# Twelve weight preparations of a hybrid layer's mixer and second feed-forward net done during the first feed-forward net and kept in DRAM

## The chip, the cores and the metric

The kernel runs as one program on one core of a Trainium2 chip. The metric is the device time of one execution in microseconds, the median over several executions. The engines named below are TensorE (PE, its weight loads PEld), VectorE (DVE), ScalarE (ACT), GpSimd (POOL) and SyncE (SP), which here only issues DMAs. Each engine works through its own instructions in order, and waits at an instruction whose inputs or buffers are not ready.

## The reference, cut to what matters

One layer works on 528 tokens (16 learned ones and 512 of the input) of width 1024: half a SwiGLU feed-forward step of width 2816, a mixer with two branches (a diagonal state-space model, and attention over 128 selected keys), and another half feed-forward step. Everything is fp32.

```python
def swiglu(x, w_gate, w_up, w_down):
    return (jax.nn.silu(x @ w_gate) * (x @ w_up)) @ w_down

hn = rms_norm(h, ff1_norm_pre[l])
h = h + 0.5 * rms_norm(swiglu(hn, ff1_w_gate[l], ff1_w_up[l], ff1_w_down[l]), ff1_norm_post[l])
hn = rms_norm(h, mix_norm_pre[l])
proj = hn @ w_in[l]                      # 1024 x 3784
u_a, q_idx, k_idx, w_idx, q, k, v, gates = split_columns(proj, IN_SPLITS)
y_a = s5_mixer(u_a, ...)                 # state-space scan, GELU, sigmoid GLU
y_b = dsa_mixer(q_idx, k_idx, w_idx, q, k, v, rel_bias, top_k)   # index scores, top 128 keys, attention
g = jax.nn.sigmoid(gates).reshape(bsz, L, N_BRANCH, D_MODEL)
merged = g[:, :, 0] * (y_a @ w_branch_a[l]) + g[:, :, 1] * (y_b @ w_branch_b[l])
h = h + rms_norm(merged @ w_out[l], mix_norm_post[l])
hn = rms_norm(h, ff2_norm_pre[l])
h = h + 0.5 * rms_norm(swiglu(hn, ff2_w_gate[l], ff2_w_up[l], ff2_w_down[l]), ff2_norm_post[l])
```

## The kernel before

**Three products for one.** Every fp32 product runs as three f16 products. An operand is written as a high part (rounded to f16) and a low part (what the rounding left, again f16), and `mm3` (L313 to L319) adds high times high, high times low and low times high in PSUM. Weights come from DRAM as fp32 and are split on the chip. `unit` (L260 to L273) does it for one unit of weights, 1024 x 256 values: SP loads 1 MB into a staging buffer `ws` (two buffers), ACT writes the high part scaled by 256 into a tile `wh` (L271), DVE the low part (L272), both in four pieces of 128x512 or fewer larger ones. Six `wh` tiles of 1 MB (high and low) exist; a tile comes free when PE has used it.

**Stages.** The first net's gate and up products (22 column tiles of 128, in pairs that share a unit of each matrix) run from some 10 us to 272 us, its down product until about 390 us. In them `hook` is called several times in a tile, and each call from tile 4 on does one step of the set-up of attention and state-space model (L788 to L813). Then comes the mixer (to about 752 us): the projections of the index, key and value columns, and then `filler`, which gives PE the work of two query units, eight gate units, the GLU, both branch products, while the index scores, top-128 selection (DVE, L1335 and L1336), state-space scans (DVE L1244, POOL L1251, PE L1238 to L1263) and attention (PE L1304, POOL L1363, ACT L1371, PE L1379, DVE L298, PE L1411) run beside it. PE's own order is written out by hand there; the other engines' order is set by priorities when the program is built.

**The second net** (`ff2`, from about 752 us) runs its first two column tiles with plain units, and the other twenty in ten pairs with Strassen's seven products instead of eight. A pair's weights arrive as `raw` (128x4x512 of gate and of up; L95). From three of the four blocks come high and low parts `wr` (L103, L108), from sums of the blocks (`sums`, L113 to L115) high and low parts `whs`. The activations take the same treatment: `comb` (L1554 to L1572) and its parts `tops` (L298, L296). A product (L137) fills a PSUM bank with two 256-token halves; ACT copies banks out (L153: `p`, `u`).

**Queue order.** All weight loads, the copies between partitions (`kx`, `kk`, L949), the state-space model's loads (`U` L1218, `E` L1228, `R` L1230, `Tm` L1256, `Gm` L1258), the bias table `BV` (L1046) and the store `Ud` (L1028) are issued by SP, in one order.

Of the kernel before, what the change touches and what calls it, by code (L numbers as in the profile page):

```python
# [17 lines left out]
KT = 8  # L18
# [42 lines left out]
def layouts(inputs):  # L61


    import numpy as np
    out = {}
    for key in ("gate", "up"):
        w = np.asarray(inputs["ff2_w_" + key])[0].reshape(2, 4, 128, NF, 128)
        f1, f2 = w[:, :, :, 2:12], w[:, :, :, 12:22]
        q = np.stack([f2[1], f1[0], f1[1], f2[0]])
        out["ff2_%s_pairs" % key] = np.ascontiguousarray(q.transpose(3, 2, 0, 1, 4)).reshape(10, 128, 4, 512)  # L70
    return out


class Strassen:
# [14 lines left out]
    def load(self, p):  # L89
        l, nc = self.l, self.l.nc  # L90
        with l.hi():
            for i, w in enumerate(self.w):
                r = l.wst.tile([128, 4, 512], F32, tag="ws", name="raw")
                s = l.SG.tile([128, 4, 512], F32, tag="sums", name="sums", bufs=2)
                nc.sync.dma_start(r, w[p])  # L95
                self.raw[p, i], self.sums[p, i] = r, s
                self.ops[p, i] = (l.SG.tile([128, 2, 3, 512], F16, tag="wr", name="wr", bufs=4),
                                  l.whl.tile([128, 2, 4, 512], F16, tag="wh", name="whs"))

    def hi(self, p, i, b):  # L100

# [118 lines left out]
class Layer:  # L220
# [39 lines left out]
    def unit(self, w, k0, nk, c0, n, ctx=None, lead=None, parts=1, pool=None, early=False):  # L260

        nc = self.nc
        with ctx or self.hi():
            st = self.staging(early, nk, n)
            nc.sync.dma_start(st, w[k0 * 128:(k0 + nk) * 128, c0:c0 + n].rearrange("(k p) n -> p k n", p=128))
            wt = (pool or self.whl).tile([128, 2, nk, n], F16, tag="wh", name="wh")
        with ctx or (self.tc.high_priority(offset=lead) if lead else self.hi()):
            step = nk // parts
            for k in range(0, nk, step):
                ks = slice(k, k + step)  # L270
                nc.scalar.activation(wt[:, 0, ks], st[:, ks], AF.Copy, scale=WS)  # L271
                nc.vector.scalar_tensor_tensor(wt[:, 1, ks], st[:, ks], WS, wt[:, 0, ks], op0=MUL, op1=SUB)  # L272
        return wt  # L273

    def staging(self, early, nk, n):
# [587 lines left out]
    def ff1(self):  # L863
        with self.prio(SP0):
            self.start()

        def fillers():
            yield
            self.attn_setup()
            yield  # L870
            yield from self.ssm_setup()
        fill = fillers()

        def hook(ft):
            if ft >= F0:
                next(fill, None)
        with self.tc.manual_schedule(engines={mybir.EngineType.PE}) if MAN else nullcontext():
            self.ff1_gate_up(hook)
        for _ in fill:
            pass  # L880
        self.hn2 = self.hn
        self.ff1_down()
# [5 lines left out]
    def mid(self):  # L888
# [186 lines left out]
        def filler():  # L1075
            nonlocal tags

            for j2 in range(2):
                with self.after(self.norm_end) if j2 < NE else nullcontext():
                    u = self.unit(w, 0, KT, C_Q + j2 * 256, 256, lead=LEAD, parts=4)  # L1080
                for hs in REAL:
                    yield from qproj(u, 2 * j2, hs, self.q)
            tags = cycle(TG2)
            for i, t_ in enumerate((T0, T1)):
                for j4 in range(4):
                    if 4 * i + j4 == 7:
                        yield from glu()
                    with self.after(self.norm_end) if 4 * i + j4 + 2 < NE else nullcontext():
                        u = self.unit(w, 0, KT, C_G + i * D + j4 * 256, 256, lead=LEAD, parts=4)
                    for j in range(2):  # L1090
                        p = yield from proj_steps(u, unit_cols(u, j), (NM, T))
                        with self.hi():
                            s.activation(t_[:, 2 * j4 + j], p, AF.Tanh, scale=0.5 * IWS)
# [408 lines left out]
    def ff2(self):  # L1502
# [7 lines left out]

        ug, uu = [self.unit(w, 0, KT, 0, 256, parts=F2P) for w in (wg, wu)]
        sg.load(0)
        manual = lambda: self.tc.manual_schedule(engines={mybir.EngineType.PE, mybir.EngineType.DVE, mybir.EngineType.Activation})
        pgs = [[self.ps("ps"), self.ps("sc")] for j in range(2)]

# [7 lines left out]
        for j in range(2):  # L1523
            prod(j, 128, SEQ)
        with self.prio(WP), self.after(self.wout_marks[0]), manual():
            for i in range(2):
                sg.hi(0, i, 0)
            sg.lo(0, 0, 0)
            for _ in self.wout_T(0):
                pass  # L1530
            sg.lo(0, 1, 0)
        self.sctx.close()
        self.lctx_close()
        self.kctx, self.cctx = ExitStack(), ExitStack()
# [48 lines left out]
            self.split(t_[:, 0], t_[:, 1], sl)  # L1583
        sg.rest = rest
        with manual():
            sg.add(0, 0)
            sg.hi(0, 0, 1)
            sg.add(0, 1)
            sg.hi(0, 1, 1)
            sg.load(1)  # L1590
            combine(0, 1)
            for i in range(2):
                sg.lo(0, i, 1)
            for j in range(2):
                prod(j, 0, 128)
                s.activation(sl[:, j], pgs[j][0], AF.Silu, scale=IWS)
# [67 lines left out]

SSMW = 512
SH = 2
NS=((0,1),1,1,3,3)
NE = 3
LN=0b0110110
# [63 lines left out]
```

## Time and profile before

| what | value |
|---|---|
| device time, median of 3 runs | 1098.4 us (1096.31 to 1099.3) |
| profiled execution, device time | 1100.52 us |
| its span (first to last instruction) | 1098.7 us |
| PE busy | 1046.6 us (95%), 8382 matmuls |
| DVE, ACT, POOL busy | 755.1 us (69%), 471.0 us (43%), 173.4 us (16%) |
| mean granted PE clock | 0.98 |
| chain that ended last | PE 76%, DVE 14%, ACT 4%, DMA 2% |
| bytes moved by DMA | 135.37 MB, mean 123 GB/s |

The profiled execution is 1.82 us longer than its span. Busy shares are means over stages with different limits; a matmul's end is modelled, and a busy PE can be one at the lower of its two clocks (1.2 instead of 2.4 GHz), which the granted clock beside a stretch shows: 1.00 is full, 0.5 half. An idle time in a row stands in brackets with what ended it.

### The profile page before, as it was taken

Reading aid. Unit: us, or ns where it says so; the run is one execution under the profiler, and the core shown is the slowest. Engines: PE = TensorE matmul, PEld = TensorE weight load, DVE = VectorE, ACT = ScalarE, POOL = GpSimd, SP = SyncE. Lnnn points to the kernel's source line nnn. Section 1 sums busy time; section 2 is a strip of 40 time slices with the busy share of each in tenths; the row PEclk is TensorE's granted clock in tenths of the full one; section 3 lists DMA queues with packets and bytes.
Section 4 is the critical chain, followed back from the end, with each engine's and each line's share of the span. In section 5 each row is a group of like instructions: output and inputs, shape, how many; then the busy total and the mean of one; then the engine's idle time right before and its main releaser. Section 6 shows DMA issues by size and latency. Waiting matters only on the chain.

```text
span 1098.7 us, 20502 instructions
## 1 busy us (share of the span) xinstructions
PE 1046.6 (95%) x8382; PEld 790.3 (72%) x8382; DVE 755.1 (69%) x1598; ACT 471.0 (43%) x854; POOL 173.4 (16%) x258
## 2 busy tenths in 40 slices
PE   7999999999999999889998999999889999999996
PEld 6888888888888988676654456565678888864443
DVE  7749766678222585599987986579979999952222
ACT  6634333333222265555656553334445555632200
POOL 4400133300000231046430223210000000001000
PEclk9999999999999999899998999999889999999999
DMA  8654454433333055946313225121323333365011
GB/s 274 184 157 144 137 176 142 140 102 127 123 106 97 1 152 169 272 155 165 126 57 99 69 78 180 51 87 69 116 78 116 116 116 116 116 219 203 20 39 39
DMA packets 94478, 135.37 MB, mean 123 GB/s; under 512 B 17336, under 2 KB 69192, under 8 KB 91824
## 3 DMA queue, kind: packets, MB, share of 16 engines
q1 hardware_dynamic: 88704, 119.92, 34.3%
q0 software_dynamic: 5056, 13.08, 4.1%
q8 instruction: 66, 1.08, 0.4%
q10 hardware_dynamic: 624, 1.06, 0.3%
q14 instruction: 28, 0.23, 0.1%
HBM read 118.45 MB, written 19.05 MB: 125 GB/s over the span
## 4 chain that ended last, share of the span: by engine, by line
PE 76%; DVE 14%; ACT 4%; DMA 2%; issue 2%; POOL 1%; SPq 1%; DVEq 0%; ACTq 0%; POOLq 0%
PE psps L319 11%; PE psps L317 11%; PE psps L315 11%; PE psps L137 9%; PE scps L315 7%; PE scps L319 7%; PE scps L317 7%; PE ptps L137 4%; DVE wh L272 3%; PE avps L137 2%; DVE iacc L1336 1%; PE ptps L319 1%; PE ptps L317 1%; PE ptps L315 1%; DVE m L1335 1%
## 5 line engine op out<-in xcount | busy, mean ns | idle before, releaser
L272 DVE SCALAR_TENSOR_TENSOR wh<-ws,wh 128x512 f16<-128x512 f32 (+2 forms) x176 | 167.2, 986 | 91.5 <-ACT wh L271 91.0
L319 PEld LDWEIGHTS <-wh 128*128 128x128 f16 x1616 | 159.3, 99 | 45.5 <-issue 4.5
L315 PEld LDWEIGHTS <-wh 128*128 128x128 f16 x1616 | 159.2, 99 | 42.0 <-issue 6.0
L317 PEld LDWEIGHTS <-wh 128*128 128x128 f16 x1616 | 159.4, 99 | 37.8 <-issue 4.5
L271 ACT ACTIVATE wh<-ws 128x512 f16<-128x512 f32 (+2 forms) x176 | 134.4, 826 | 104.7 <-PE scps L319 54.6
L315 PE MATMUL psps<-hn,wh 128*128 128x256 f16 (+2 forms) x640 | 166.0, 302 | 4.2 <-DVE kk L300 1.9
L317 PE MATMUL psps<-hn,wh 128*128 128x256 f16 (+2 forms) x640 | 166.5, 302 | 1.1 <-POOL hn L298 0.6
L319 PE MATMUL psps<-hn,wh 128*128 128x256 f16 (+2 forms) x640 | 166.5, 301 | 0.0
L137 PEld LDWEIGHTS <-whs 128*128 128x128 f16 x960 | 95.0, 99 | 18.0 <-issue 5.9
L137 PEld LDWEIGHTS <-wr 128*128 128x128 f16 x720 | 71.8, 100 | 13.5 <-issue 3.7
L315 PE MATMUL scps<-hn,wh 128*128 128x272 f16 (+1 forms) x344 | 68.7, 276 | 0.0
L317 PE MATMUL scps<-hn,wh 128*128 128x272 f16 (+1 forms) x344 | 68.6, 276 | 0.0
L319 PE MATMUL scps<-hn,wh 128*128 128x272 f16 (+1 forms) x344 | 68.1, 276 | 0.0
L137 PE MATMUL psps<-tops,whs 128*128 128x256 f16 x480 | 57.8, 279 | 5.5 <-ACT u L153 5.5
L108 DVE SCALAR_TENSOR_TENSOR whs<-sums,whs 128x2048 f16<-128x2048 f32 x20 | 45.7, 2291 | 3.6 <-ACT whs L103 3.6
L510 ACT ACTIVATE sl<-scps 128x272 f32<-128x272 f32 (+1 forms) x40 | 14.4, 386 | 66.5 <-PE scps L319 66.5
L103 ACT ACTIVATE whs<-sums 128x2048 f16<-128x2048 f32 x20 | 38.1, 1904 | 10.2 <-DVE sums L115 10.2
L1363 POOL TENSOR_TENSOR BM<-BV,iacc 128x272 f32<-128x272 f32 (+1 forms) x32 | 28.8, 909 | 85.0 <-DVE asm L1369 73.5
L315 PE MATMUL psps<-h,wh 128*128 128x256 f16 (+1 forms) x176 | 41.5, 276 | 0.0
L317 PE MATMUL psps<-h,wh 128*128 128x256 f16 (+1 forms) x176 | 41.5, 276 | 0.0
L319 PE MATMUL psps<-h,wh 128*128 128x256 f16 (+1 forms) x176 | 41.5, 276 | 0.0
L319 PE MATMUL scps<-h,wh 128*128 128x256 f16 (+1 forms) x176 | 41.5, 276 | 0.0
(412 smaller groups left out, 2125.5 us busy)
## 6 DMA issues: line engine op xcount, KB each, us to landing
ws<-in_ff_w_down_dram SPq DMA_DIRECT2D x18, 1024.0 KB, 5.2
ws<-in_w_in_dram SPq DMA_DIRECT2D x14, 1024.0 KB, 6.6
ws<-in_ff_w_gate_dram SPq DMA_DIRECT2D x10, 1024.0 KB, 5.4
ws<-in_ff_w_up_dram SPq DMA_DIRECT2D x10, 1024.0 KB, 6.2
raw<-ff_gate_pairs SPq DMA_DIRECT2D x10, 1024.0 KB, 4.8
raw<-ff_up_pairs SPq DMA_DIRECT2D x10, 1024.0 KB, 4.9
ws<-in_w_out_dram SPq DMA_DIRECT2D x4, 1024.0 KB, 5.1
ws<-in_ff_w_down_dram SPq DMA_DIRECT2D x4, 768.0 KB, 4.7
```

The costliest lines, as they stand in the source:

```text
L103: self.l.nc.scalar.activation(self.ops[p, i][b][:, 0], src[:, 0:3] if b == 0 else src, AF.Copy, scale=WS)
L108: self.l.nc.vector.scalar_tensor_tensor(o[:, 1], src[:, 0:3] if b == 0 else src, WS, o[:, 0], op0=MUL, op1=SUB)
L137: mm(out, a, b[:, kt], start=first and i == kt == x == 0, stop=kt == 3 and x == 2, skip_group_check=True)
L271: nc.scalar.activation(wt[:, 0, ks], st[:, ks], AF.Copy, scale=WS)
L272: nc.vector.scalar_tensor_tensor(wt[:, 1, ks], st[:, ks], WS, wt[:, 0, ks], op0=MUL, op1=SUB)
L315: mm(p, a[0], bh, start=first, stop=False)
L317: mm(p, a[0], bl, start=False, stop=False)
L319: mm(p, a[1], bh, start=False, stop=last)
L510: s.activation(sl[:, a:b], p[:, :b - a], AF.Silu, scale=IWS)
L1335: v.max(m8, work)
L1336: v.match_replace(work, m8, work, -3e38)
L1363: nc.gpsimd.tensor_add(BM[:, :w], self.BV[:, h, NA - w:], madd[:, f:])
```

## The change

Ten units of the mixer's weights (two of the query, eight of the gates; `AHEAD`), until now loaded and split in the mixer, and the first Strassen pair of the second net (gate and up: blocks and sums), until now loaded, summed and split at that net's start, are loaded and split during the first net's gate and up products. `ahead_steps` does it, one step at every second call of `hook` from tile 4 on: load into a buffer `wa` (two buffers, in the pool `EX` that holds the first net's early units), split by ACT and DVE in pieces of 128x1024 (128x512 for `wr`), and store the f16 parts to a tile `wd` in DRAM. The ten units come from a new input, `ahead`, that holds each of them as 8 KB in one piece for each partition. All twelve loads and fourteen stores are issued by SP; a load is issued only after the weight load that the program issued last before it (`sp_mark`).

In the mixer `kept_unit` takes the place of `unit`: one load of 1 MB f16 from `wd` into a `wh` tile, and no work of ACT or DVE. In the second net `load(0)` loads the four prepared tiles (two `wr` of 0.75 MB, two `whs` of 1 MB), and the splits and sums of pair 0 go. `load(1)`, the raw weights of the next pair, is issued directly behind it.

```diff
@@ layouts
-    out = {}
+    w = np.asarray(inputs["w_in"])[0].reshape(KT, 128, -1)
+    out = {"ahead": np.stack([w[:, :, c:c + 256].transpose(1, 0, 2) for c in AHEAD])}
@@ Strassen.load
             for i, w in enumerate(self.w):
+                self.ops[p, i] = (l.SG.tile([128, 2, 3, 512], F16, tag="wr", name="wr", bufs=4),
+                                  l.whl.tile([128, 2, 4, 512], F16, tag="wh", name="whs"))
+                if p == 0:
+                    for b in range(2):
+                        nc.sync.dma_start(self.ops[p, i][b], l.kept[i, b])
+                    continue
...
-                self.ops[p, i] = (l.SG.tile([128, 2, 3, 512], F16, tag="wr", name="wr", bufs=4),
-                                  l.whl.tile([128, 2, 4, 512], F16, tag="wh", name="whs"))
@@ Layer.unit
-            nc.sync.dma_start(st, w[k0 * 128:(k0 + nk) * 128, c0:c0 + n].rearrange("(k p) n -> p k n", p=128))
+            self.sp_mark = nc.sync.dma_start(st, w[k0 * 128:(k0 + nk) * 128, c0:c0 + n].rearrange("(k p) n -> p k n", p=128))
@@ new
+    def ahead_steps(self):
...
+        def halves(dst, src, step):
+            for a in range(0, src.shape[1], step):
+                ks = slice(a, a + step)
+                nc.scalar.activation(dst[:, 0, ks], src[:, ks], AF.Copy, scale=WS)
+                nc.vector.scalar_tensor_tensor(dst[:, 1, ks], src[:, ks], WS, dst[:, 0, ks], op0=MUL, op1=SUB)
+
+        def keep(key, t_):
+            self.kept[key] = d = self.dp.tile(list(t_.shape), F16, tag=str(key), name="wd")
+            nc.sync.dma_start(d, t_)
+
+        def stage(shape, src=None, dt=F32):
+            t_ = self.EX.tile(shape, dt, tag="wh", name="wa")
+            if src is not None:
+                with self.after([self.sp_mark]):
+                    nc.sync.dma_start(t_, src)
+            return t_
+        for i, c in enumerate(AHEAD):
+            st = stage([128, KT, 256], self.I["ahead"][i])
+            wt = stage([128, 2, KT, 256], dt=F16)
+            halves(wt, st, 4)
+            keep(c, wt)
+            yield
+        v = nc.vector
+        for i, key in enumerate(("gate", "up")):
+            r = stage([128, 4, 512], self.I[f"ff2_{key}_pairs"][0])
+            wr = stage([128, 2, 3, 512], dt=F16)
+            halves(wr, r[:, 0:3], 1)
+            keep((i, 0), wr)
+            yield
+            t_ = stage([128, 4, 512])
+            v.tensor_add(t_[:, 0:2], r[:, 3:4].to_broadcast([128, 2, 512]), r[:, 0:2])
+            v.tensor_add(t_[:, 2], t_[:, 0], r[:, 1])
+            v.tensor_add(t_[:, 3], t_[:, 2], r[:, 2])
+            yield
+            whs = stage([128, 2, 4, 512], dt=F16)
+            halves(whs, t_, 2)
+            keep((i, 1), whs)
+            yield
+
+    def kept_unit(self, c):
+        with self.hi():
+            wt = self.whl.tile([128, 2, KT, 256], F16, tag="wh", name="wh")
+            self.nc.sync.dma_start(wt, self.kept[c])
+        return wt
@@ ff1
         def hook(ft):
             if ft >= F0:
                 next(fill, None)
+                if next(calls) % 2:
+                    next(ahead, None)
@@ filler
-                    u = self.unit(w, 0, KT, C_Q + j2 * 256, 256, lead=LEAD, parts=4)
+                    u = self.kept_unit(C_Q + j2 * 256)
...
-                        u = self.unit(w, 0, KT, C_G + i * D + j4 * 256, 256, lead=LEAD, parts=4)
+                        u = self.kept_unit(C_G + i * D + j4 * 256)
@@ ff2
         sg.load(0)
+        sg.load(1)
...
-            for i in range(2):
-                sg.hi(0, i, 0)
-            sg.lo(0, 0, 0)
             for _ in self.wout_T(0):
                 pass
-            sg.lo(0, 1, 0)
...
-            sg.add(0, 0)
-            sg.hi(0, 0, 1)
-            sg.add(0, 1)
-            sg.hi(0, 1, 1)
-            sg.load(1)
             combine(0, 1)
-            for i in range(2):
-                sg.lo(0, i, 1)
@@ constants
+AHEAD = [C_Q, C_Q + 256] + [C_G + i * 256 for i in range(8)]
```

Line numbers of the changed kernel are 5 higher than before in the Strassen class, 55 in `split` (L298 is L353), and 59 to 62 higher in the mixer and the second net.

The first place is SP's order where the last projections end, about 438 to 460 us of the profile before. `Ud`, `BV`, `R`, `Tm` and `Gm` serve the state-space model and the attention bias, `kx` and `kk` are copies to other partitions, `U` the model's inputs, `ws` a raw weight unit. Before:

```order
L1046 DMA BV<-Vr 128x8x272
L1028 DMA Ud<-uT 128x528
L1230 DMA R<-Rd 128x528
L1256 DMA Tm<-Td 128x512
L1258 DMA Gm<-Gd 128x512
L949 DMA kx<-kx 64x2x256
L265 DMA ws<-in_w_in_dram 128x8x256
L949 DMA kk<-kk 64x2x256
L1218 DMA U<-Ud 16x32x66 x8
```

After (`wh<-wd` is the load of a prepared unit):

```order
L1318 DMA Tm<-Td 128x512
L1320 DMA Gm<-Gd 128x512
L1090 DMA Ud<-uT 128x528
L1108 DMA BV<-Vr 128x8x272
L1090 DMA Ud<-uT 128x528
L327 DMA wh<-wd 128x4096
L1011 DMA kx<-kx 64x2x256
L1011 DMA kk<-kk 64x2x256
L1280 DMA U<-Ud 16x32x66 x5
L327 DMA wh<-wd 128x4096
```

The raw load that stood behind `kx` is gone and a prepared unit's load stands in front of it; `R`, `Tm` and `Gm` stand further ahead, `BV` nearer, and another prepared unit's load stands between the loads of `U`.

The second place is DVE's order in the mixer, about 476 to 485 us: `Vbd` of the state-space model, the selection (`MAX`, `MATCH_REPLACE` on `iacc`), the query's evacuation `q`, the low part of a weight unit, and the scan `SZ`. Before:

```order
L1167 TENSOR_TENSOR Vbd<-ptps,mask 128x512
L1325 MEMSET iacc 64x64
L1335 MAX m_5939<-iacc 128x8
L961 SCALAR_TENSOR_TENSOR q<-psps,q 64x256
L272 SCALAR_TENSOR_TENSOR wh<-ws,wh 128x512
L1336 MATCH_REPLACE iacc<-m_5939,iacc 128x528
L272 SCALAR_TENSOR_TENSOR wh<-ws,wh 128x512 x3
L1335 MAX m_5970<-iacc 128x8
L961 SCALAR_TENSOR_TENSOR q<-psps,q 64x256
L1336 MATCH_REPLACE iacc<-m_5970,iacc 128x528
L961 SCALAR_TENSOR_TENSOR q<-psps,q 64x256
L1244 SCALAR_TENSOR_TENSOR SZ<-dec,SZ 128x264
```

After:

```order
L1387 MEMSET iacc 64x64
L1229 TENSOR_TENSOR Vbd<-ptps,mask 128x512
L1397 MAX m_6064<-iacc 128x8
L1023 SCALAR_TENSOR_TENSOR q<-psps,q 64x256
L1398 MATCH_REPLACE iacc<-m_6064,iacc 128x528
L1023 SCALAR_TENSOR_TENSOR q<-psps,q 64x256
L1397 MAX m_6086<-iacc 128x8
L1398 MATCH_REPLACE iacc<-m_6086,iacc 128x528
L1397 MAX m_6141<-iacc 128x8
L1398 MATCH_REPLACE iacc<-m_6141,iacc 128x528
L1306 SCALAR_TENSOR_TENSOR SZ<-dec,SZ 128x264
```

The four passes over a weight unit (rows `wh<-ws,wh`) are gone from in front of the scan, and three more steps of the selection stand there.

The third place is DVE's order at the start of the second net, from about 770 us. Before:

```order
L108 SCALAR_TENSOR_TENSOR wr<-raw,wr 128x1536
L298 TENSOR_TENSOR hf<-ptps,hf 128x4x128 x2
L108 SCALAR_TENSOR_TENSOR wr<-raw,wr 128x1536
L1554 TENSOR_TENSOR raw<-hf 128x4x128
L298 TENSOR_TENSOR tops<-comb,tops 128x4x128 x5
L1565 SCALAR_TENSOR_TENSOR comb<-comb,raw 128x4x128
L298 TENSOR_TENSOR tops<-comb,tops 128x4x128
L108 SCALAR_TENSOR_TENSOR whs<-sums,whs 128x2048 x2
L1568 TENSOR_TENSOR comb<-raw 128x4x128
L113 TENSOR_TENSOR sums<-raw 128x1024
L298 TENSOR_TENSOR tops<-comb,tops 128x4x128
```

After:

```order
L353 TENSOR_TENSOR hf<-ptps,hf 128x4x128 x2
L1613 TENSOR_TENSOR raw<-hf 128x4x128
L353 TENSOR_TENSOR tops<-comb,tops 128x4x128 x2
L1624 SCALAR_TENSOR_TENSOR comb<-comb,raw 128x4x128
L353 TENSOR_TENSOR tops<-comb,tops 128x4x128 x4
L1627 TENSOR_TENSOR comb<-raw 128x4x128
L353 TENSOR_TENSOR tops<-comb,tops 128x4x128
L113 SCALAR_TENSOR_TENSOR wr<-raw,wr 128x1536 x2
L1613 TENSOR_TENSOR raw<-hf 128x4x128
L185 TENSOR_TENSOR C<-avps,p_9557 128x512
L118 TENSOR_TENSOR sums<-raw 128x1024
L1631 SCALAR_TENSOR_TENSOR comb<-comb,raw 128x4x128
```

The passes that write the first pair's `wr` and `whs` are gone; the first `comb` stands behind two `tops` passes instead of five, and the passes over `wr` that remain are the second pair's.

## Rows read from the trace of the kernel before

**Rows 1.** Windows of the span: start:end, length, busy per engine, granted clock, DMA share, GB/s.

```profile
60.00:192.00 132.00, 132.00 (x1160) 112.05 (x1158) 88.99 (x234) 47.38 (x100) 25.49 (x43) 1.00 0.47 149
385.00:466.00 81.00, 74.19 (x720) 64.31 (x719) 53.23 (x127) 45.73 (x110) 13.21 (x18) 0.96 0.71 199
466.00:568.00 102.00, 94.33 (x696) 66.29 (x694) 98.07 (x211) 57.82 (x134) 49.13 (x72) 0.98 0.44 135
568.00:640.00 72.00, 62.45 (x366) 32.80 (x367) 59.59 (x139) 42.28 (x83) 15.84 (x22) 0.91 0.28 82
...
752.00:806.00 54.00, 43.68 (x340) 31.68 (x339) 45.11 (x71) 25.74 (x32) 0.00 (x0) 0.87 0.25 90
```

**Rows 2.** PE's waits, 466 to 568 us: waited for, total us, times, longest.

```profile
PE ptps L1263 <- POOL SZ L1251: 2.6, 1, 2.6
PE ptps L1262 <- DVE PT L298: 2.3, 2, 1.4
PE ptps L1262 <- DVE Vbd L1167: 0.7, 1, 0.7
PE psps L315 <- DVE q L961: 0.6, 1, 0.6
```

**Rows 3.** Timeline of DVE, 476 to 490 us: start, us, what.

```profile
479.10 3.54 DVE L272 SCALAR_TENSOR_TENSOR wh<-ws,wh 128x512 f16<-128x512 f32 x3
...
485.00 0.71 DVE L1244 TENSOR_TENSOR_SCAN SZ<-dec,SZ 128x264 f32<-128x264 f32 x1
```

**Rows 4.** Groups by line, 466 to 568 us: busy, mean ns, idle before.

```profile
L272 DVE SCALAR_TENSOR_TENSOR wh<-ws,wh 128x512 f16<-128x512 f32 x24 | 20.8, 911 | 0.0
```

**Rows 5.** PE's waits, 385 to 466 us.

```profile
PE scps L1304 <- DMA kx<-kx: 2.1, 1, 2.1
PE psps L315 <- DVE kk L300: 1.9, 2, 1.4
```

**Rows 6.** Chain that ended last, 436 to 452 us: start, us, what.

```profile
438.90 2.50 DVE wh L272 x4
...
442.00 7.57 DMA kx<-kx
```

**Rows 7.** PE's waits, 752 to 806 us.

```profile
PE psps L137 <- ACT u L153: 5.0, 1, 5.0
PE psps L137 <- ACT sl L1596: 3.6, 1, 3.6
```

**Rows 8.** Timeline of DVE, start of the second net.

```profile
770.39 1.75 DVE L108 SCALAR_TENSOR_TENSOR wr<-raw,wr 128x1536 f16<-128x1536 f32 x1
...
780.76 4.49 DVE L108 SCALAR_TENSOR_TENSOR whs<-sums,whs 128x2048 f16<-128x2048 f32 x2
...
796.80 0.68 DVE L1572 SCALAR_TENSOR_TENSOR comb<-comb,raw 128x512 f32<-128x512 f32 x1
```

**Rows 9.** Timeline of ACT, start of the second net.

```profile
779.49 0.63 ACT L296 ACTIVATE tops<-comb 128x512 f16<-128x512 f32 x1 [4.15 <-DVE comb L1565]
...
797.52 0.63 ACT L296 ACTIVATE tops<-comb 128x512 f16<-128x512 f32 x1 [3.30 <-DVE comb L1572]
798.12 1.91 ACT L103 ACTIVATE whs<-sums 128x2048 f16<-128x2048 f32 x1
```

**Rows 10.** Windows: two after PE's waits, one full of DVE, one full of DMA.

```profile
781.00:788.00 7.00, 5.92 (x29) 4.12 (x29) 5.99 (x4) 2.11 (x5) 0.00 (x0) 0.51 0.02 4
798.00:805.50 7.50, 4.93 (x26) 3.61 (x26) 2.89 (x3) 2.52 (x4) 0.00 (x0) 0.54 0.39 140
82.50:110.00 27.50, 27.50 (x246) 23.84 (x245) 27.09 (x118) 12.56 (x27) 0.81 (x1) 1.00 0.44 143
432.50:447.50 15.00, 13.64 (x124) 11.88 (x123) 6.44 (x13) 7.09 (x17) 0.45 (x2) 1.00 1.03 359
```

**Rows 11.** Groups by line, first net (0 to 385 us).

```profile
L272 DVE SCALAR_TENSOR_TENSOR wh<-ws,wh 128x512 f16<-128x512 f32 x72 | 46.8, 688 | 11.1 <-ACT wh L271 11.0
```

**Rows 12.** Groups by line, mixer (385 to 760 us).

```profile
L272 DVE SCALAR_TENSOR_TENSOR wh<-ws,wh 128x1024 f16<-128x1024 f32 x8 | 9.9, 1258 | 2.5 <-ACT wh L271 2.5
```

More of the change, by code (lines that the diff above doesn't have):

```diff
@@ L272, in unit @@
                 nc.vector.scalar_tensor_tensor(wt[:, 1, ks], st[:, ks], WS, wt[:, 0, ks], op0=MUL, op1=SUB)
+        return wt
+    def ahead_steps(self):
+        nc = self.nc
+        self.kept = {}
+        def halves(dst, src, step):
[38 more added lines that the diff above has]
+            self.nc.sync.dma_start(wt, self.kept[c])
         return wt
@@ L872, in ff1 @@
         fill = fillers()
+        ahead = self.ahead_steps()
+        calls = iter(range(1000))
         def hook(ft):
@@ L879, in ff1 @@
         for _ in fill:
+            pass
+        for _ in ahead:
             pass
```

## The prediction

> **What bounds the kernel now.** I read the windows of the span first, because they show which engine fills which stage [rows 1]. Between 60 and 192 us PE never stops at full clock, and DVE has 132 - 89.0 = 43.0 us free: there PE alone sets the time. From 466 to 568 us DVE is busy 98.1 of 102 us, and PE, which still has work, stands for 102 - 94.3 = 7.7 us. From 752 to 806 us PE stands for 54 - 43.7 = 10.3 us. So a pass taken off DVE is worth nothing in the first net and may be worth something in the other two. Second come PE's waits in these stretches. In the mixer they end with DVE or with POOL's part of the scan [rows 2]; at the second net's start they end with ACT, in two gaps of 3.6 and 5.0 us [rows 7]. Third come the timelines of DVE and ACT at these waits, which show what is queued ahead of the instruction that PE waits for [rows 3, 8, 9], and last the granted clock behind the gaps: 0.51 and 0.54 in the two stretches after the second net's gaps, which is about the lower of its two levels (1.2 of 2.4 GHz) [rows 10].
>
> **Added in the first net.** Ten units in two pieces of 128x1024 give 20 passes on DVE, the two `whs` 4 more: 24 x 1.258 = 30.2 us [rows 12]. The two `wr` give 6 passes of 128x512 at 0.688 = 4.1 us [rows 11]. The sums, for each matrix one addition of 128x1024 and two of 128x512, I take at the same two durations: 2 x (1.258 + 2 x 0.688) = 5.3 us. Together 39.6 us. The steps run over about 16 tiles, some 165 us, and of the 39.6 us about 33 fall between 60 and 192 us, where 43.0 are free [rows 1]. ACT gets 30 passes, at no more than DVE's durations 34 us, against 132 - 47.4 = 84.6 us free in that window alone. DMA gets 12 loads of 1 MB and 14 stores, 12.6 and 14.2 MB: 26.7 MB in 165 us are 162 GB/s on top of 149 [rows 1], 311 in all, while 359 were moved for 15 us on end in the mixer [rows 10]. PE gets nothing. What hides all this is that PE's tiles need DVE only now and then: between 82.5 and 110 us DVE is busy 27.1 of 27.5 us, and PE does not stop once [rows 10]. If the cover is gone, PE stands for a silu or an evacuation that comes late. No row shows both loads at once. The lower bound is 0 (PE is never idle there, so nothing can be gained), the upper some two late steps of 3 us each, 6; I take 1, near the row in which DVE is full and PE doesn't wait.
>
> **Mixer, 385 to 466 us.** Five of the ten units are split here. One stall of PE, 1.4 us of the 1.9 us for `kk` [rows 5], has four passes of L272, 2.50 us, directly before it on the chain [rows 6]. Without them `kk` is ready at the pace of ACT; I take 0.9 off this stall and 0.5 off a smaller one of the same kind, -1.4. The wait for `kx` (2.1 us) stays: it is a DMA that landed 7.57 us after its issue [rows 5, 6], and in SP's order a 1 MB load of a prepared unit now stands directly ahead of it, where the raw load stood behind. Bounds: at 359 GB/s [rows 10] the 1.05 MB take 2.9 us, so at worst +2.9; at best the wait goes, -2.1. The three `R`, `Tm` and `Gm` loads that were issued just before it stand further ahead now, so I take 0.
>
> The Trainium skill (DMA: Bandwidth & Descriptors, Queues, rings and completion order) says that each DMA engine takes the descriptors of a queue in ring order, so the megabyte ahead would be moved before `kx`. By that rule alone the sum would be 2.9 us higher; the trace shows the long landing of `kx` behind the `BV` load, which agrees, but not which share each transfer ahead of it has.
>
> **Mixer, 466 to 568 us.** Of 24 passes of L272 (20.8 us) [rows 4] 20 belong to kept units and go; four are the GLU's. 20 x 0.911 = 18.2 us, by which DVE's 98.1 fall to 80, while PE's own work takes 94. DVE no longer is the bound. How this reaches PE is seen at the largest wait, 2.6 us for `SZ` [rows 2]: three passes of L272, 3.54 us, stood on DVE between 479.1 and 482.6, ahead of the scan at 485.0 [rows 3]. The four waits sum to 6.2 us. I leave 0.7 of them, since a transpose must still follow its exponential, and take 5.5. The clock granted was 0.98 of 102 us, so 2.0 us went with it, after the gaps; these go too. -7.5. Bounds: 0 (other waits replace them all) and -9.7 (all of PE's idle time and the clock).
>
> **568 to 752 us** keep their work: the splits there belong to the branch and output units, which are not prepared. 0; a gain is possible through a lead of DVE (below).
>
> **Second net's start.** The first gap ends with `sl` on ACT [rows 7], which follows a `tops` that had waited 4.15 us for `comb` L1565 [rows 9]. On DVE two passes over `wr` of 1.75 us stood ahead of that `comb` [rows 8], as the order before shows. Without them it ends 3.5 us earlier, and the gap of 3.6 closes. The second gap, 5.0 us, ends with `u`, which follows the second pair's `whs` (1.91) and a `tops` that waited 3.30 for `comb` L1572 at 796.80 [rows 8, 9]. Ahead of that on DVE the two `whs` passes go, 4.49 us [rows 8]. So `u`, which could start at 798.12 + 1.91 = 800.0, moves ahead by 3.5 + 4.5 = 8.0, to 792.0. PE went on about half a microsecond behind it, so its gap of 5.0 began at 795.5; freed of the first gap (3.6) and of its slow stretch (5.92 x 0.49 = 2.9) [rows 10], it gets there at 795.5 - 6.5 = 789.0. A gap of 2 to 3.5 us is left, since what remains ahead of `u` is the second pair's own work. PE thus goes on 8.0 us earlier, or 9.5 if the shorter `tops` queue in the new order helps as well. After a gap of two the slow stretch behind it (4.93 x 0.46 = 2.3) gets shorter by some 0.5. I take -9.0; bounds -13 (both gaps of 8.6 and both slow stretches of 5.2 gone, less 0.8 of smaller ones that appear) and -3 (the second gap grows by what the first loses and its stretch stays slow, leaving 2.9). The loads must be there: 3.7 MB from 752 us on, at 359 GB/s 10.2 us, and the first is needed at about 778.
>
> **Sum.** +1 - 1.4 + 0 - 7.5 + 0 - 9.0 = -16.9. The profiled execution took 1100.52 us, so 1083.6 for its like; it is 2.1 above the median of the runs, 1098.4, from which 1081.5 follows. I say **1082 us**.
>
> **Rivals.**
> *Only the second net gains.* In the mixer the waits move: DVE's selections follow one another through scores that come from PE, and with L272 gone PE may stand for POOL's part of `SZ` or for `kx` instead. For it speaks that the largest wait in rows 2 names POOL; against it that DVE was full. 1098.4 + 1 - 9.0 = 1090 us.
> *DVE's lead carries on.* DVE saves 18 us before 568 and PE takes 7.5 of them; if the rest lets the attention's exponentials and transposes come early, the 72 - 62.5 = 9.5 us of PE's idle time between 568 and 640 and its clock's 0.09 x 72 = 6.5 go [rows 1]: 16 us more, 1066 us. Against it: these waits lie in a chain that begins with PE's own scores.
> *Slower: late steps in the first net.* ACT and DVE take their passes in order. A pass over `wa` that waits for its load stands ahead of a tile's silu, and the silu frees PE's bank. A tile takes 11 us (132 us hold 1160 matmuls of 96 a tile), so half a tile, 5.5 us, is cover. A load that lands as late as `kx` did, 7.57 us [rows 6], lets PE stand for 2.1 us, and in the proportion of the gap of 3.6 with its slow stretch of 2.9 that costs 3.7. The gains are 17.9 without this term; from 6 such steps of 16 on the kernel is slower by over 0.3%, and with 12 it takes 1098.4 - 17.9 + 44.4 = 1125 us. For it: SP issues the loads one after another with the stores, and a store that waits for DVE holds the next load back. Against it: loads of 1 MB and passes over them already run in this stretch with PE never idle.
> *No change.* The loads from DRAM wait on SP for `wh` tiles that PE frees late, and hold `kx`, `U`, `Tm` and `Gm` and the second net's weights back by what DVE gains: about 1098 us. The order of SP speaks for it, and that PE stands for `kx` already; against it, that SP had such waits for staging buffers before.
>
> **How the numbers follow.** Forecast 0.56, its own range 1074 to 1089; only the second net 0.18; DVE's lead 0.12; late steps 0.08; no change 0.06. A range of 1066 to 1094 leaves out the last two cases, 0.14, and a little of the edges. About 0.3% (3.3 us) is what a measurement of this kernel can tell from no change. Faster by more: 0.56 + 0.18 + 0.12 = 0.86, less 0.02 for the first net's cost rising to its bound while the mixer gains nothing, 0.84. Within: 0.08. Slower: 0.08.
>
> **What would show it.** In the profile after: PE busy without a gap from 60 to 385 us (first step), DVE near 122 of 132 us there; the wait for `kk` under 1 us and that for `kx` about 2; DVE near 80 of 102 us in the stretch that answers to 466 to 568, with PE's waits for `SZ` and `PT` nearly gone; no wait for `sl`, and one of 2 to 3.5 us for `u`, in the second net. I am wrong if PE waits on evacuations in the first net, if its waits in the mixer keep their sum under other names, or if the second net starts with a wait for `wr<-wd`.

## The result, and the profile after

The changed kernel takes 1092.5 us (median of 19 executions, 1086.8 to 1096.4), the kernel before on the same chips 1102.1 us. The ratio is 0.9921 with a 95% interval of 0.9901 to 0.9941: 8.7 us faster, where 16.9 were forecast. About half of the gain is missing; the sign and the range held. (Two of the 19 executions of the kernel before took 2189 and 6158 us; without them its median is 1099.3 us, and the ratio leaves them out.)

First the windows of the kernel after that answer to [rows 1]; the columns are the same (length; busy of PE, PEld, DVE, ACT, POOL; granted clock, DMA share, GB/s).

```profile
60.00:192.00 132.00, 126.53 (x1103) 106.36 (x1101) 105.65 (x243) 66.99 (x121) 21.52 (x36) 1.00 0.86 293
385.00:466.00 81.00, 75.71 (x742) 66.27 (x741) 41.37 (x126) 31.95 (x80) 11.98 (x17) 0.96 0.66 184
466.00:568.00 102.00, 95.23 (x683) 69.22 (x682) 76.26 (x173) 48.56 (x117) 43.17 (x67) 0.92 0.45 137
568.00:640.00 72.00, 63.13 (x396) 33.69 (x394) 61.05 (x149) 41.43 (x78) 17.30 (x22) 0.98 0.26 81
752.00:806.00 54.00, 50.22 (x404) 36.40 (x403) 41.37 (x80) 21.82 (x35) 0.00 (x0) 0.97 0.36 127
```

DVE has what the change promised: 76.3 instead of 98.1 us in the third row. PE has not: it now stands 5.5 us between 60 and 192 us, where it never stood before, and in the third row its idle time fell only from 7.7 to 6.8 us, with a granted clock of 0.92 instead of 0.98. The last row is as forecast: 3.8 us idle instead of 10.3, clock 0.97 instead of 0.87.

The windows of two kernels that run apart don't hold the same work. Three waits of PE that both have serve as marks: the first `kk` (start of the mixer), a product over the last attention block (`ybh`), and a `u` behind the second net's start. The kernel before (start, duration, what, and in brackets the idle time ahead of it):

```profile
410.10 0.28 PE L315 MATMUL psps<-hn,wh 128*128 128x256 f16 x1 [0.57 <-DVE kk L300]
...
723.28 0.22 PE L315 MATMUL psps<-ybh,wh 128*128 128x128 f16 x1 [0.72 <-DVE y L1480]
...
821.65 1.58 PE L137 MATMUL psps<-tops,whs 128*128 128x256 f16 x13 [0.47 <-ACT u L153]
```

and after:

```profile
417.88 0.28 PE L370 MATMUL psps<-hn,wh 128*128 128x256 f16 x1 [0.58 <-DVE kk L355]
...
729.01 0.22 PE L370 MATMUL psps<-ybh,wh 128*128 128x128 f16 x1 [0.72 <-DVE y L1542]
...
817.59 1.58 PE L142 MATMUL psps<-tops,whs 128*128 128x256 f16 x13 [0.48 <-ACT u L158]
```

At the first mark the kernel is 7.8 us late, at the second 5.7, at the third 4.1 us early. So this execution lost 7.8 us in the first net, gained 2.1 in the mixer and 9.8 at the second net's start. In the forecast these were +1, -8.9 and -9.0. (It took 1096.4 us, the longest of the 19; the second profile below gives +7.3, -6.4 and -11.5.)

**The first net.** PE's waits from 60 to 385 us (waited for, total, times, longest), of which the kernel before has none:

```profile
PE avps L849 <- ACT B L867: 4.6, 4, 1.9
PE avps L849 <- DVE A L845: 0.8, 1, 0.8
```

They make 5.4 of the 7.8 us; the rest stays open. One of them on the timelines of SP, PE, ACT and PE again:

```profile
144.04 0.43 SPq L299 DMA_DIRECT2D wa<-ahead  x1
```

```profile
145.81 1.05 PE L861 MATMUL avps<-B,A 128*16 128x128 f32 x8
```

```profile
154.53 2.00 ACT L288 ACTIVATE wa<-wa 128x1024 f16<-128x1024 f32 x2 [6.02 <-DMA wa<-ahead]
156.44 0.57 ACT L867 ACTIVATE B<-avps 16x512 f32<-16x512 f32 x1
```

```profile
157.06 0.66 PE L849 MATMUL avps<-ident,A 128*128 128x128 f32 x4 [1.89 <-ACT B L867]
```

The load into `wa` was issued at 144.0 us. ACT stood at the pass over it from 148.5 until the load had landed at 154.5, 10.5 us after its issue. Behind the pass in ACT's order is `B`, the copy out of PSUM of the state-space model's set-up. Its input was there from 146.9 us on, when PE's product (L861) ended, but it ran only when the pass was done. PE's next set-up step, transposes (L849) into the only bank of their kind (`av`), stands in PE's order between the tile's matmuls, was reached at 155.2 us and waits for `B`. So PE stops for the set-up, not for an operand of its tile. At all four waits for `B` a pass over `wa`, for whose load ACT had stood 2.7 to 6.0 us, ends directly before `B` on ACT. The fifth wait is DVE's: its sum `A` (L845) at 119.5 us comes behind two passes over `wa` (2.35 us).

**The mixer.** PE's waits from 440 to 560 us after, for [rows 2, 5]:

```profile
PE scps L1366 <- DMA kx<-kx: 4.1, 1, 4.1
PE psps L370 <- DVE q L1023: 3.6, 1, 3.6
PE ptps L1324 <- DVE PT L353: 1.4, 1, 1.4
PE ptps L1300 <- DMA wh<-wd: 1.3, 1, 1.3
```

The waits for `SZ`, `Vbd` and `kk` that were to go are gone or small, but `kx` has doubled, and one wait of 3.6 us for `q` has come. On the chain `kx` landed later after its issue than before [rows 6]:

```profile
446.56 10.65 DMA kx<-kx
```

**The second net.** Both waits of [rows 7] are answered by one line (waits of PE, 752 to 820 us); no wait for `sl` is left:

```profile
PE psps L142 <- ACT u L158: 2.5, 2, 2.0
```

### The profile page after: what moved, and what is told of

Same layout as the page of the kernel before. It is cut to its first block, busy times and chain, and to the rows that moved or that the text cites. A ratio compares the mean times of both kernels' runs of the same rounds, so it can differ in the third digit from the quotient of the medians.

```text
span 1094.6 us, 20517 instructions
## 1 busy us (share of the span) xinstructions
PE 1044.6 (95%) x8382; PEld 790.5 (72%) x8382; DVE 747.5 (68%) x1584; ACT 471.0 (43%) x840; POOL 170.3 (16%) x258
## 4 chain that ended last, share of the span: by engine, by line
PE 62%; DVE 12%; ACT 3%; DMA 2%; issue 2%; POOL 1%; SPq 0%; DVEq 0%; ACTq 0%; POOLq 0%
PE psps L374 9%; PE psps L372 9%; PE psps L370 9%; PE psps L142 9%; PE scps L372 5%; PE scps L374 5%; PE scps L370 5%; PE ptps L142 4%; PE avps L142 2%; DVE wh L277 2%; DVE iacc L1398 1%; DVE m L1397 1%; PE scps L1366 1%; DMA kx<-kx 1%; PE ptps L374 1%
## 5 line engine op out<-in xcount | busy, mean ns | idle before, releaser
L277 DVE SCALAR_TENSOR_TENSOR wh<-ws,wh 128x512 f16<-128x512 f32 (+2 forms) x136 | 136.7, 1036 | 79.3 <-ACT wh L276 79.2
L276 ACT ACTIVATE wh<-ws 128x512 f16<-128x512 f32 (+2 forms) x136 | 112.6, 883 | 89.2 <-PE scps L374 55.1
L289 DVE SCALAR_TENSOR_TENSOR wa<-wa 128x1024 f16<-128x1024 f32 (+1 forms) x30 | 32.5, 1113 | 29.7 <-ACT wa L288 29.7
L288 ACT ACTIVATE wa<-wa 128x1024 f16<-128x1024 f32 (+1 forms) x30 | 27.4, 963 | 41.8 <-DMA wa<-ahead 27.4
L113 DVE SCALAR_TENSOR_TENSOR whs<-sums,whs 128x2048 f16<-128x2048 f32 x18 | 41.2, 2292 | 3.6 <-ACT whs L108 3.6
L370 PE MATMUL scps<-h,wh 128*128 128x256 f16 (+1 forms) x176 | 41.4, 276 | 0.0
L372 PE MATMUL scps<-h,wh 128*128 128x256 f16 (+1 forms) x176 | 41.4, 276 | 0.0
```

The lines of the kernel that those rows point to most:

```text
L113: self.l.nc.vector.scalar_tensor_tensor(o[:, 1], src[:, 0:3] if b == 0 else src, WS, o[:, 0], op0=MUL, op1=SUB)
L288: nc.scalar.activation(dst[:, 0, ks], src[:, ks], AF.Copy, scale=WS)
L289: nc.vector.scalar_tensor_tensor(dst[:, 1, ks], src[:, ks], WS, dst[:, 0, ks], op0=MUL, op1=SUB)
L370: mm(p, a[0], bh, start=first, stop=False)
L372: mm(p, a[0], bl, start=False, stop=False)
```

## The experiments

Each kernel is compared with executions of the kernel before on the same chip. In the expectations ORDER is the theory that the lost gain lies in what stands ahead of what; its rivals have other names from case to case.

**Once more.** The changed kernel as it is, for a second profile.

> The changed kernel once more, unchanged. Theory ORDER (the lost gain is a matter of what stands ahead of what in the engines' and SP's fixed orders): the same waits come back, four or five for the set-up's copies B and A between 110 and 190 us (5 us in all), kx about 4 us, q about 3.6 us with a stretch at half the clock behind it, u about 2 us; ratio to the kernel before 0.990 to 0.994. Theory CHANCE (the profiled execution, 1096.4 us, was one of the slow ones): some of these waits are absent or the slow stretch behind q is shorter than 5 us, and the profiled execution takes 1087 to 1093 us.

Measured: 1090.3 us, ratio 0.9904 (0.9876 to 0.9932); the profiled execution 1089.9. The waits for `B` and `A` came back (3.4 and 1.8 us), `kx` with 4.1, `q` with 3.6, `u` with 2.0. What differs is the clock behind the wait for `q`. Windows of the first profile after that wait:

```profile
500.00:504.00 4.00, 2.81 (x7) 1.02 (x8) 3.81 (x8) 0.67 (x2) 1.73 (x3) 0.52 0.65 244
504.00:508.00 4.00, 4.00 (x18) 3.49 (x17) 3.83 (x9) 1.14 (x3) 0.00 (x0) 0.50 0.02 4
508.00:512.00 4.00, 4.00 (x16) 2.76 (x16) 1.79 (x5) 1.26 (x4) 2.49 (x4) 0.50 0.43 141
```

and of the second:

```profile
500.00:504.00 4.00, 2.47 (x7) 0.96 (x8) 3.77 (x10) 0.98 (x3) 2.06 (x3) 0.74 0.73 274
504.00:508.00 4.00, 4.00 (x29) 3.38 (x28) 3.83 (x9) 1.19 (x4) 0.54 (x1) 0.84 0.15 44
508.00:512.00 4.00, 4.00 (x20) 1.85 (x19) 2.73 (x6) 1.80 (x4) 2.58 (x5) 1.00 0.44 153
```

The same gap of 3.6 us was followed by 12 us at half the clock in one execution; in the other the first two windows, 0.74 and 0.84, make some 3.4 us at half the clock, an estimate from these two means. The mixer, between the first two marks (306.8 instead of 313.2 us), gains 6.4 us in the second profile. The second net's start gains 11.5 us there and 9.8 in the first profile, in which the clock from 792 to 800 us was 0.82 (1.00 in the second). ORDER has the waits and the ratio right, and CHANCE the profiled time and the shorter slow stretch. The waits are the program's; a part of the spread from 1087 to 1096 us is how long the clock stays down.

**The first net's part alone.**

```diff
-                    u = self.kept_unit(C_Q + j2 * 256)
+                    u = self.unit(w, 0, KT, C_Q + j2 * 256, 256, lead=LEAD, parts=4)
...
-                        u = self.kept_unit(C_G + i * D + j4 * 256)
+                        u = self.unit(w, 0, KT, C_G + i * D + j4 * 256, 256, lead=LEAD, parts=4)
@@ Strassen.load and ff2: as before the change
```

> Everything that the change adds in the first net (loads, passes, stores, in the changed kernel's order) and nothing that it takes off: mixer and second net load and split their own weights as before, and what was stored is not used. Theory ORDER: the waits for the set-up's copies come back (about 5 us) and the first net ends some 7 us late: ratio to before 1.004 to 1.008. The prediction's term (1 us, at most 6): ratio 1.000 to 1.003.

Measured: 1107.8 us, ratio 1.0065 (1.0044 to 1.0086): +7.2 us. Its waits of PE from 60 to 385 us:

```profile
PE avps L845 <- ACT B L863: 3.0, 2, 2.0
PE avps L845 <- DVE A L841: 1.6, 1, 1.6
```

Behind the second wait for `B`, 1.95 us long, the clock fell as well:

```profile
158.00:162.00 4.00, 4.00 (x23) 2.87 (x22) 4.00 (x8) 2.24 (x5) 1.86 (x3) 0.57 0.68 231
```

This prices the term that the prediction put at 1 us and bounded at 6. The waits are 4.6 us of it. By the marks the loss is where the work was added: +8.1 us at the first, -0.3 in the mixer. The second net's start, with the code of the kernel before, took 1.7 us less than there, so that stretch differs by as much from one profile to another without the change.

**Only the ten units.** `ahead_steps` without its second loop; `Strassen.load` and `ff2` as before.

> Only the ten mixer units are prepared ahead; the second net's first pair is loaded, summed and split there, as before. Theory ORDER: the second net loses its 9.8 us again, the first net keeps three of its waits for B and A (about 4 us), the mixer gains some 2 us: ratio to the kernel before 0.998 to 1.004. Theory of the prediction: the mixer gains 8.9 and the first net loses 1: ratio 0.993.

Measured: 1097.9 us, ratio 0.9967 (0.9948 to 0.9987), between the two theories: a little better than ORDER's nearer end, 0.998, and short of the prediction's 0.993. The first mark comes 6.5 us late, the second 0.5, so the mixer gains 6.0, where ORDER had 2 and the prediction 8.9. At the second net's start both of PE's waits are back:

```profile
PE psps L138 <- ACT u L154: 5.3, 1, 5.3
PE psps L138 <- ACT sl L1654: 3.6, 1, 3.6
```

**Only the first pair.** `AHEAD = []`, and `unit` in the mixer.

> Only the second net's first pair is prepared ahead (six steps); the mixer's units are loaded and split there, as before. Theory ORDER: second net -9.8 us, first net 0 to +2, mixer 0: ratio 0.991 to 0.993, as good as the whole change. If the mixer's part of the change were worth 9 us, this would be slower than the whole change by 0.5% or more.

Measured: 1093.8 us, ratio 0.9930 (0.9903 to 0.9956), as theory ORDER had it: the first pair alone, two of the twelve preparations, is not to be told from the whole change. Its first mark is 2.7 us late and its second 3.8, and the second net's start gains 9.9 us, as in the whole change. The ten units alone had lost in the first net (6.5 us) what they gained in the mixer (6.0).

**ACT's passes behind the set-up's copy.** The same loads, passes and stores; an edge puts both halves of a pass over a prepared unit, ACT's and DVE's, behind the set-up's last copy.

```diff
+        self.kmark = None
+
         def halves(dst, src, step):
+            with self.after([self.kmark] if self.kmark else []):
+                halves_(dst, src, step)
...
-            s.activation(kev, p[:M], AF.Copy)
+            self.kmark = s.activation(kev, p[:M], AF.Copy)
```

> The whole change, but ACT's passes over a prepared unit are issued behind the copy B that the set-up emitted last, instead of ahead of it; loads, stores and passes are the same. Theory ORDER: the waits for B between 110 and 190 us (5 us idle) fall under 1 us, and the kernel is 5 to 7 us faster than the changed one: ratio to before 0.984 to 0.988. Theory TRAFFIC (the 27 MB more of DMA delay what the first net needs, whatever the order): the time stays within 1 us of the changed kernel's, ratio 0.990 to 0.994.

Measured: 1084.2 us, ratio 0.9845 (0.9812 to 0.9878). The traffic is that of the changed kernel and PE doesn't stop in this window:

```profile
60.00:192.00 132.00, 132.00 (x1161) 112.39 (x1159) 109.75 (x251) 66.90 (x121) 23.31 (x39) 1.00 0.83 285
```

Its only wait of PE from 60 to 385 us is:

```profile
PE avps L867 <- ACT A L856: 0.9, 1, 0.9
```

ACT still stands at passes over `wa` for the ten units' loads, 19.8 us from 60 to 240 us (24.3 in the changed kernel), but nothing that PE needs soon is behind them. So theory TRAFFIC falls: 285 GB/s in that window cost PE nothing by themselves. The edge moved more than it names, since PE's order in the first net is set by priorities when the program is built: the set-up's transposes stand 11.5 to 12.3 us apart on PE (12.3 before the change) instead of 8.4 to 15.6. How much of the gain beyond the named waits comes from that was not separated. This version beats both kernels. Its gain, 17 us, is close to the forecast of 16.9 in part by luck: by the marks its parts are +2.4, -6.9 and -11.5 us, where +1, -8.9 and -9.0 were forecast.

**Loads behind `kx` and `U`.** On top of that kernel; the gate units' loads get an edge behind `kk`'s copy and the last `U` load.

```diff
-                        u = self.kept_unit(C_G + i * D + j4 * 256)
+                        with self.after([m for m in (self.kk_mark, self.u_mark) if m]):
+                            u = self.kept_unit(C_G + i * D + j4 * 256)
```

> On top of the kernel in which ACT's passes stand behind the set-up's copy: the loads of the eight prepared gate units are issued by SP behind the copies kx and kk and behind all eight loads U, instead of one ahead of kx and one between the U loads. Theory ORDER: kx lands 7 to 8 us after its issue instead of over 10, its wait falls from 3.9 to 1 to 2 us, the wait of 2.0 us at the first product of U to under 1; with the slow stretch behind the first, 3 to 5 us less than 1084, so 1079 to 1081. Theory BANDWIDTH (these bytes must be moved in the same microseconds in any order): one wait is replaced by another for a gate unit, and the time stays at 1083 to 1085.

Measured: 1083.4 us, ratio 0.9833 (0.9809 to 0.9857), not to be told from 0.9845. `kx`'s wait fell from 3.9 to 2.9, that at the first product of `U` from 2.0 to 0.7:

```profile
PE psps L376 <- DVE q L1029: 3.5, 1, 3.5
PE scps L1374 <- DMA kx<-kx: 2.9, 1, 2.9
...
PE ptps L1308 <- DMA wh<-wd: 0.7, 1, 0.7
```

The copy itself came as ORDER had it, 7.4 us after its issue (7 to 8 expected) instead of 11.1 without the edit; PE, whose order moved too, was at its product 3 us earlier and so still waited:

```profile
440.25 0.60 SPq L1017 DMA_DIRECT2D kx<-kx  x1
447.67 0.55 PE L1374 MATMUL scps<-kx,qx 128*128 128x272 f16 x2 [2.86 <-DMA kx<-kx]
```

In its chain a store `Ud` takes `kx`'s place, with 10.2 us to its landing. The profiled execution is 4 us shorter than that of the kernel without the edit (span 1078.7 for 1082.7), but the median moves by 0.8. By the times BANDWIDTH is nearer, by the landing and the wait for `U` ORDER; what the edit is worth stays open.

**The scan's copies on POOL.**

```diff
-            s.activation(S[0:64, 1], S[64:128, 0], AF.Copy, scale=-1.0)
-            s.activation(S[64:128, 1], S[0:64, 0], AF.Copy)
+            nc.gpsimd.tensor_scalar(S[0:64, 1], S[64:128, 0], -1.0, None, op0=MUL)
+            nc.gpsimd.tensor_copy(S[64:128, 1], S[0:64, 0])
```

> On top of the same kernel: the two copies of the scan's state SZ that follow the scan are made by POOL instead of ACT. In ACT's order they stand ahead of a query's evacuation q and wait there for DVE's scan. Theory ORDER: the wait of 3.6 us for q falls to 0.5 to 1.5 us and the slow stretch behind it goes: 3 to 5 us less than 1084. Theory DVE (DVE is full with the selection between 480 and 500 us, and q waits for DVE itself): the wait stays at 3 us or more, and the time within 1 us.

Measured: 1084.1 us, ratio 0.9849 (0.9823 to 0.9876). The time is as theory DVE had it; the wait for `q` fits neither theory. It shrinks by a microsecond and PE stands for `SZ` instead:

```profile
PE psps L376 <- DVE q L1029: 2.6, 1, 2.6
...
PE ptps L1331 <- POOL SZ L1319: 1.7, 2, 1.0
```

What is left of the wait can be read on ACT and DVE. ACT's half of `q` is done at 490.3 us and DVE's half begins 3.0 us later, behind selection passes and the scan, without idle time on DVE between them:

```profile
489.91 0.38 ACT L1028 ACTIVATE q<-psps 64x256 f16<-64x256 f32 x1 [0.92 <-PE psps L380]
491.97 0.70 DVE L1312 TENSOR_TENSOR_SCAN SZ<-dec,SZ 128x264 f32<-128x264 f32 x1
493.30 0.42 DVE L1029 SCALAR_TENSOR_TENSOR q<-psps,q 64x256 f16<-64x256 f32 x1
```

**Both edits.**

> Both edits together with the passes behind the set-up's copy. If both theories ORDER hold, 6 to 9 us less than 1084: 1075 to 1078, ratio to before 0.976 to 0.979. If BANDWIDTH and DVE hold: 1083 to 1085.

Measured: 1084.9 us, ratio 0.9846 (0.9824 to 0.9867): no gain, as BANDWIDTH and DVE had it.

**Half the selection.** `for r in range(8 if b == 3 else (out or TOPK) // 8)`, which leaves out 64 of the 128 keys for the last 128 queries.

> On top of the kernel with ACT's passes behind the set-up's copy: the selection for the last 128 queries makes 8 of its 16 rounds (64 keys instead of 128 chosen), some 12 us of DVE less between 475 and 505 us. Theory DVE (the selection fills DVE there and q waits behind it): the wait of 3.6 us for q falls to under 1 us, DVE has idle time from 488 to 500 us, and the time falls by 3 us or more under 1084. Theory CHAIN (q waits for ACT and the scan, not for DVE's work): the wait stays at 2.5 us or more.

Measured: 1087.0 us, ratio 0.9873 (0.9845 to 0.9901). The wait for `q` is still 2.9 us:

```profile
PE psps L376 <- DVE q L1029: 2.9, 1, 2.9
```

DVE is busy 3.8 of 4 us from 488 to 492 and not at all from 496 to 500: the rounds that stand ahead of `q` in its order still stand there, and it runs dry afterwards. How much DVE has to do in all is not what holds `q`, but what stands ahead of `q` there; theory DVE falls in the form in which I had put it, and the wait is as CHAIN had it. Of the 2.9 us by which its profiled execution is longer, 1.7 lie at the second net's start, with a clock of 0.79 from 784 to 792 us (1.00 in the kernel without the edit); the 1.9 us in the mixer are not explained.

**More of PE's other work beside the selection.** `RF = 1.8` for 1.4.

> On top of the same kernel: PE gets 1.8 instead of 1.4 us of projection work for each round of the selection in the order that is written out for it, so that its work before 505 us is longer. If DVE's selection sets the pace there, the wait for q shrinks by what PE has more to do, and PE stands later instead, between 568 and 640 us, for the exponentials: time 1082 to 1087. If q's wait is a chain's latency: wait unchanged, time 1084.

Measured: 1089.6 us, ratio 0.9892 (0.9866 to 0.9918). The wait for `q` falls to 0.7 us, but from 560 to 640 us PE stands 9.5 instead of 3.7 us for the exponentials, and 4.1 for the index scores' copies:

```profile
PE ptps L1447 <- ACT Pt L1439: 9.5, 3, 4.5
PE scps L1372 <- ACT rl L1386: 4.1, 3, 2.2
```

The waits move as expected, but the time is longer than either theory allowed. PE's projections cover one wait or the other; spent early, they are missing late.

## Why the prediction was wrong, step by step

**Views.** That ACT and DVE bound the second net's start was read rightly. That DVE bounds 466 to 568 us was read off its busy share and held only in part: with 76.3 instead of 98.1 us of work on DVE, PE's idle time fell from 7.7 to 6.8. That PE alone sets the time from 60 to 192 us was right for the kernel before, and the wrong conclusion was drawn from it.

**First net: +1 forecast, +7.2 measured** (the first net's part alone). This is the step that failed: "the upper some two late steps of 3 us each, 6; I take 1", on the ground that PE's tiles need DVE only now and then. The load on the engines was sized well: DVE's added passes take 37.7 us in all (39.6 forecast), though its 105.7 us in the window are short of 122, and ACT has 67.0 there. A late evacuation was named as the danger and priced at next to nothing. What I did not look at is that PE's own order there also holds the set-up's transposes, which wait for an ACT copy through a single bank. That copy had 8.3 us, from 146.9 to 155.2; ACT's wait for the load and its pass took them and 1.9 us more. Since it is an evacuation too, the sign of being wrong that the prediction had named for this stretch came. I had asked what PE's tiles wait for, not what stands on PE. With the passes behind `B`, the same work and the same traffic take 6 to 8 us less than the changed kernel by the ratios (0.9845 for 0.9904 and 0.9921), and no wait for `B` is left.

**The rival of late steps** had the right mechanism, a pass that waits for its load in ACT's order, at the wrong victim: no silu or evacuation of a tile's products made PE wait, but the set-up's copy. Three to six waits, for 16 steps, cost PE up to 2.0 us each, where it asked for 3.7 each with a slow clock. The granted clock stayed at 1.00 in both profiles of the changed kernel; with the first net's part alone it fell to 0.57 for 4 us once.

**Mixer: -8.9 forecast, -2.1, -6.4 and -6.9 in the profiles** of the changed kernel, of its second execution and of the kernel with the passes behind `B`. The waits for `kk`, `SZ` and `Vbd` went as said. Against that stand `kx`, +2.0 us, and `q`, +3.0. For `kx` I took 0 between -2.1 and +2.9. The landing grew from 7.57 to 10.65 us [rows 6], 3.1 us, near the upper bound, which was the time of the megabyte ahead at 359 GB/s. With the load moved behind it the landing fell back, from 11.1 to 7.4 us, and the wait by 1.0. The Trainium skill (DMA: Bandwidth & Descriptors, Queues, rings and completion order) says that descriptors on a DMA engine are taken in ring order; the trace agrees, with 10.65 us behind the load and 7.4 ahead of it. For `q` I wrote that DVE "no longer is the bound", and left out that the selection, which waits for nothing, moves up into the room that L272 leaves, so that DVE is as busy between 480 and 500 us as before (19.1 of 20 us, 19.3 before). Of the wait for `q` the ACT copies account for 1 us (the copies on POOL); in that kernel's trace the rest is DVE's order, selection passes and the scan ahead of `q`. No run moved these, so the rest is read and not tested. PE's waits from 385 to 568 us thus kept most of their sum under other names: all of them make 13.0 us before and 12.0 after. Some of the mixer's gain lies from 568 to 640 us instead, where I had 0: the wait for `Pt` there and behind fell from 5.9 to 3.7 us, and the clock rose from 0.91 to 0.98.

**Second net: -9.0 forecast, -9.8, -11.5 and -11.5 measured** between the second and third mark, in the same three profiles; two profiles with the second net's old code differ by 1.7 us there too. No wait for `sl`, and 2.0 us for `u`, as written.

**Sum.** Taken alone, the first net's part is +0.65%, and the whole change -0.79 to -0.96%; without the waits for `B` it is -1.55%, where the forecast was -1.54% (16.9 of 1100.5). Of the forecast's error of 8 us some 6 are the first net's term. The rest is the mixer's shortfall, 2 us and more, of which the second net's better gain hid a part.

## What to carry to other kernels

Before work is put beside a full PE, list everything in PE's own order in that stretch, not only its main products, and ask of each what it waits for: here a side chain through one PSUM bank and an ACT copy lost its 8.3 us of slack to a single pass. A pass that waits for a DMA held everything behind it on its engine (ACT stood 6.0 us), and an edge that puts it behind the short copies cost nothing here and was worth 0.6 to 0.8%. And a gain is to be priced by whose work moves up into the freed room: here the selection did, and the wait only changed its name.

## What the runs showed that was not expected

The same program with the same gap of 3.6 us on PE ran on at half the clock for 12 us in one execution and for some 3.4 us (the estimate above) in another; a single profile can be off by several microseconds in one stage for this reason alone. Three waits of 1.2 to 1.9 us between full tiles in the first net left the granted clock at 1.00 in the changed kernel, while 0.57 for 4 us followed one of 1.95 us in the run of the first net's part. And with the added traffic a unit of gate or up weights landed later, though neither made PE wait. From the page of the kernel after (KB each, median us from issue to landing), with `wa` beside them:

```profile
ws<-in_ff_w_gate_dram SPq DMA_DIRECT2D x10, 1024.0 KB, 7.4
ws<-in_ff_w_up_dram SPq DMA_DIRECT2D x10, 1024.0 KB, 8.8
wa<-ahead SPq DMA_DIRECT2D x10, 1024.0 KB, 7.6
```

The first two took 5.4 and 6.2 us before.
